# Root mean squares of a two-layer decoder step: column products and diagonals replaced by sums on all partitions

## The chip, the cores and the metric

The kernel runs on one core of one Trainium2 chip. The core has TensorE (PE, matrix products, results in PSUM), VectorE (DVE), ScalarE (ACT), GpSimd (POOL) and SyncE (SP, here only a queue that issues transfers). The metric is the device time of one execution in microseconds (us); lower is better.

## The reference, cut to what matters

Two layers are applied to a prompt of 1024 tokens and a sample group of 8 times 4 tokens, with a width of 1024. Each layer normalizes its input, computes one input projection, four branches (pooling, short convolution, Conformer convolution with a LayerNorm, differential attention with a norm per head), merges them, and ends in an output projection and a second norm. All norms need the same scalar for each token, one over the root of a mean square:

```python
def _rms(x, g):
    y = xf * lax.rsqrt(jnp.mean(xf * xf, axis=-1, keepdims=True) + EPS)
...
h = _rms(x, g_pre) * (1.0 + scale[:, None]) + shift[:, None]
y_c = jax.nn.silu(_layernorm(conv_c + b_cconv, g_cnorm, b_cnorm))
o = _rms(attend(q, k, v, lam), g_subln) * (1.0 - lam_init)
out = _rms(merged @ w_o, g_post)
```

## The kernel before, in words

Channels lie on the 128 partitions and tokens along the free axis, so a sum over channels runs over partitions. The 1056 tokens (1024 of the prompt, 32 of the samples) form three blocks of 352 (`TB`). A large product is 24 TensorE instructions of 128x128 by 128x352: each float32 operand is split into a high and a low part in the type float32r, and three of the four part products are summed over 8 slices of the depth (`gemm`, line 238). Results land in PSUM banks, two of them (`mm`) in the attention stages and five later, and an engine other than TensorE has to empty a bank before it is used again.

The function `drive` walks through the large products, weight unit by weight unit, three blocks each. Between them it steps generators that hold the rest: `attn` (one head of prompt attention), `decode` (two heads of sample attention), `pool`, `layernorm`. A scheduler then orders the instructions of each engine by its own estimate of durations; SP alone keeps the order of the program. Every engine works through its own row strictly in order.

`rstd_of(x, n, scale, dg, pb)` brings 1/sqrt(scale * sum + eps) of every token to all partitions. `x` holds, on each partition, partial sums of squares for `n` tokens. It is called in 38 places: 16 times at the end of the heads' attention (512 tokens each, two halves per head, line 646; I call the stretch from the last product with V to the end of these two roots an attention tail), 4 times in `decode` (64 tokens), 6 times in `layernorm` (352), 6 times behind the output projection (352, into the bank `ada`, line 1216), 3 times for the next layer's norm (352, line 1224) and 3 times at the start (`rstd_x`). It works in four steps:

- Line 349: products with the tokens as the stationary operand and one column of ones as the moving one, 4 for each call (1 in `decode`) in float32. The sums of up to 128 tokens lie on as many partitions, in a PSUM buffer `ms`, of which there are two. The trace shows each float32 product as two records.
- Lines 351 and 352: square root on ScalarE and reciprocal on VectorE, of at most 128x4 values. Lines 355 and 356 split the result into two float32r parts.
- Line 360: a diagonal matrix for each part, the identity times that column, on VectorE.
- Line 364: products of ones with the diagonals, two float32r products of the full number of columns (one float32 product in `decode` and at the start), which spread the values over all partitions, into a second `ms` buffer or into `ada`.

The caller then multiplies with the result in PSUM (lines 647, 792, 1098, 1219, and `norm_apply`). ScalarE also splits the weights (line 210) and empties banks (line 497 copies a key or query block in four pieces). It has to load another function table (`ACT_TABLE_LOAD`) when it changes between the square root and functions such as the exponential or the hyperbolic tangent. Line 1211 adds the squares behind the output projection on POOL, for the last slice on VectorE.

Of the kernel before, what the change touches and what calls it, by code (L numbers as in the profile page):

```python
# [13 lines left out]
AF = mybir.ActivationFunctionType  # L14
# [84 lines left out]
def step_kernel(ctx, tc, xT, wst, wada, kc, vc, ptab, stp, sts, stc, cT, vecs, wpool, lamqk, cst, rope,  # L99
# [58 lines left out]
    def ms(n=512):  # L158
        return psA("ms", 512)[:, 0:n]
# [161 lines left out]
    def make_A(l, k=0, n=KC):  # L321
        g = cv("g_pre", l, k, n).unsqueeze(2).to_broadcast([P, n, 9])
        ve.scalar_tensor_tensor(out=Am[:, k:k + n], in0=modT[l][:, 8 + k:8 + k + n], scalar=1.0, in1=g, op0=ALU.add, op1=ALU.mult)
# [18 lines left out]
    def rstd_of(x, n, scale, dg, pb=None):  # L342


        w = max(w_ for w_ in (P, TB // 4, 64) if n % w_ == 0)
        m = n // w
        pc = ms(m)[:w]
        for j in range(m):
            te.matmul(out=pc[:, j:j + 1], lhsT=x[:, j * w:(j + 1) * w], rhs=ones[:, 0:1], start=True, stop=True)  # L349
        r = const("rsm", 8, bufs=2)[:w, 0:m]  # L350
        sc.activation(out=r, in_=pc, func=AF.Sqrt, bias=epsc[:w], scale=scale)
        ve.reciprocal(out=r, in_=r)
        rs = [r] if len(dg) == 1 else [const(f"rsm{i}", 8)[:w, 0:m] for i in range(2)]
        if len(dg) == 2:
            ve.tensor_copy(out=R(rs[0]), in_=r)
            ve.tensor_tensor(out=R(rs[1]), in0=r, in1=rs[0], op=ALU.subtract)
        cast = R if len(dg) == 2 else lambda ap: ap
# [65 lines left out]
    def setup_lambda(l, lq):  # L423
# [9 lines left out]
        for o, name, f, w in ((0, "pool_scale", 0.5, 4), (4, "g_cnorm", 0.5, 4), (8, "b_cnorm", 0.5, 4),  # L433
                              (12, "g_subln", 0.5 * (1.0 - lam_init), 1)):
# [4 lines left out]
    def layer(l, pos, hh, hl, begun, psB):  # L439
# [120 lines left out]
        def attn(h):  # L560
# [91 lines left out]
        def decode(p):  # L652
# [137 lines left out]
            sqd, rsd = wn[:, 0:64], wn[:, 64:128]  # L790
# [650 lines left out]
```

## Time and profile before

| what | value |
|---|---|
| median of 3 runs | 3004.43 us (3002.55 to 3007.85) |
| the profiled execution's own time | 3002.23 us |
| its span, first to last instruction | 3000.4 us |
| TensorE busy | 2913.8 us, 97% of the span |
| weight loads of TensorE busy | 2781.6 us, 93% |
| VectorE, ScalarE, POOL busy | 1634.2, 970.6 and 495.1 us |
| granted TensorE clock, mean | 0.989 |

TensorE's row is nearly full, and each large product's instruction starts about 0.16 us after the one before it. A time saved on another engine counts only where TensorE waits for it. A TensorE instruction taken out of a full stretch moves everything behind it forward, unless the work behind it then has to wait for something else.

### The profile page before, as it was taken

How to read it: one execution, taken by the hardware profiler on the slowest of the kernel's cores; microseconds unless marked ns; L12 is line 12 of the kernel's file. 1: busy time of each engine (PE TensorE's matmuls, PEld its weight loads, DVE VectorE, ACT ScalarE, POOL GpSimd, SP SyncE). 2: the span in 40 equal slices, each digit the busy share in tenths (PEclk: the TensorE clock that was granted, in tenths of full speed). 3: DMA queues.
4: the chain of work that ended last, by engine and by line, in shares of the span. 5: the costliest groups of instructions: out<-in, count | busy, mean ns of one | idle time of the engine just before them, and what ended most of it. 6: DMA issues, size and time to landing. Idle time of an engine off the chain costs nothing.

```text
span 3000.4 us, 46185 instructions
## 1 busy us (share of the span) xinstructions
PE 2913.8 (97%) x18436; PEld 2781.6 (93%) x18436; DVE 1634.2 (54%) x2540; ACT 970.6 (32%) x1904; POOL 495.1 (17%) x642
## 2 busy tenths in 40 slices
PE   6999999999999999999989999999999999999998
PEld 4899889989999999999989998998899999999998
DVE  7756356577972145323487663664889522543233
ACT  4544245313112123212454551542221121322132
POOL 3221011012200111011230120101140001110123
PEclk8999999999999999999999999999999999999999
DMA  6122621362233223222321236115511221221122
GB/s 230 48 65 85 203 78 53 116 196 64 67 109 105 80 86 96 97 75 71 108 98 48 67 118 205 49 45 153 179 38 59 84 76 43 80 90 57 50 69 97
DMA packets 135961, 280.08 MB, mean 93 GB/s; under 512 B 18338, under 2 KB 88994, under 8 KB 134210
## 3 DMA queue, kind: packets, MB, share of 16 engines
q10 hardware_dynamic: 45072, 145.74, 15.9%
q1 hardware_dynamic: 79778, 90.73, 9.7%
q0 software_dynamic: 10896, 40.67, 3.6%
q8 instruction: 145, 2.38, 0.3%
q14 instruction: 70, 0.57, 0.1%
HBM read 240.73 MB, written 36.34 MB: 92 GB/s over the span
## 4 chain that ended last, share of the span: by engine, by line
PE 84%; DVE 7%; DMA 2%; issue 2%; SPq 2%; ACT 2%; POOL 0%; DVEq 0%; ACTq 0%; POOLq 0%
PE mm_t L238 45%; PE m_t L238 28%; PE s_t L238 3%; PE ms_t L238 2%; DVE acc_t L954 2%; SPq L671 1%; PE ms_t L611 1%; PE s_t L776 1%; DVE wlo_t L211 1%; PE s_t L702 1%; DVE acc_t L373 1%; DMA e_t<-in_kc_dram 1%; PE ms_t L349 1%; PE b_t L238 1%; ACT rop_t L497 1%
## 5 line engine op out<-in xcount | busy, mean ns | idle before, releaser
L238 PE MATMUL mm_t<-hh_t,whi_t 128*128 128x352 f32 x2792 | 533.3, 329 | 5.8 <-ACT hh_t L385 2.1
L238 PE MATMUL mm_t<-hh_t,wlo_t 128*128 128x352 f32 x2792 | 528.6, 327 | 0.0
L238 PE MATMUL mm_t<-hl_t,whi_t 128*128 128x352 f32 x2792 | 524.0, 325 | 0.0
L211 DVE TENSOR_TENSOR wlo_t<-wst_t,whi_t 128x1024 fp32r<-128x1024 f32 x203 | 268.5, 1329 | 455.6 <-ACT whi_t L210 455.4
L238 PEld LDWEIGHTS mm_t<-hh_t,whi_t 128*128 128x128 f32 x2792 | 458.7, 190 | 27.6 <-issue 14.6
L238 PEld LDWEIGHTS mm_t<-hh_t,wlo_t 128*128 128x128 f32 x2792 | 460.5, 189 | 9.7 <-issue 8.2
L238 PEld LDWEIGHTS mm_t<-hl_t,whi_t 128*128 128x128 f32 x2792 | 458.7, 189 | 6.7 <-issue 5.6
L954 DVE SCALAR_TENSOR_TENSOR acc_t<-uc_t,vec_t,acc_t 128x1024 f32<-128x1024 f32 x240 | 320.4, 1360 | 1.6
L1164 POOL TENSOR_TENSOR mg_t<-mg_t,th_t 128x352 f32<-128x352 f32 x144 | 144.7, 1008 | 925.8 <-DVE th_t L1163 925.7
L210 ACT ACTIVATE whi_t<-wst_t 128x1024 fp32r<-128x1024 f32 x203 | 213.3, 1056 | 246.7 <-PE mm_t L238 163.6
L238 PE MATMUL m_t<-hh_t,wlo_t 128*128 128x352 f32 x1352 | 249.7, 325 | 0.0
L238 PE MATMUL m_t<-hl_t,whi_t 128*128 128x352 f32 x1352 | 247.6, 324 | 0.0
L238 PE MATMUL m_t<-hh_t,whi_t 128*128 128x352 f32 x1352 | 246.4, 323 | 0.0
L238 PEld LDWEIGHTS m_t<-hh_t,wlo_t 128*128 128x128 f32 x1352 | 223.6, 190 | 0.9
L238 PEld LDWEIGHTS m_t<-hl_t,whi_t 128*128 128x128 f32 x1352 | 222.7, 189 | 0.0
L238 PEld LDWEIGHTS m_t<-hh_t,whi_t 128*128 128x128 f32 x1352 | 222.0, 189 | 0.1
L1072 ACT ACTIVATE th_t<-m_t 128x352 f32<-128x352 f32 x114 | 52.6, 463 | 373.4 <-PE m_t L238 362.5
L1072 ACT ACTIVATE th_t<-mm_t 128x352 f32<-128x352 f32 x78 | 35.9, 463 | 272.0 <-PE mm_t L238 240.9
L590 DVE TENSOR_REDUCE sml_t<-s_t 128x1 f32<-128x256 f32 (+7 forms) x128 | 92.4, 752 | 53.1 <-PE s_t L238 52.7
L593 ACT ACTIVATE e_t<-s_t,sml_t 128x256 f32<-128x256 f32 (+7 forms) x128 | 94.3, 744 | 69.7 <-DVE sml_t L591 39.9
L238 PE MATMUL m_t<-yh_t,whi_t 128*128 128x352 f32 x460 | 94.5, 326 | 0.0
L238 PE MATMUL m_t<-yh_t,wlo_t 128*128 128x352 f32 x460 | 93.1, 324 | 0.0
(349 smaller groups left out, 3854.0 us busy)
## 6 DMA issues: line engine op xcount, KB each, us to landing
wst_t<-in_wst_dram ACTq DMA_DIRECT2D x209, 512.0 KB, 3.6
e_t<-in_kc_dram SPq DMA_DIRECT2D x224, 128.0 KB, 3.0
e_t<-in_vc_dram SPq DMA_DIRECT2D x216, 128.0 KB, 2.6
rld_t<-ysp_t ACTq DMA_DIRECT2D x16, 528.0 KB, 4.5
wa_t<-in_wada_dram SPq DMA_DIRECT2D x16, 512.0 KB, 10.4
wlo_t<-in_wada_dram ACTq DMA_DIRECT2D x16, 512.0 KB, 3.7
whi_t<-in_wada_dram ACTq DMA_DIRECT2D x16, 512.0 KB, 4.3
x_t<-in_xT_dram SPq DMA_DIRECT2D x3, 1408.0 KB, 6.0
```

The source lines that it names most:

```text
L210: sc.activation(out=R(hi), in_=st, func=AF.Copy)
L211: (eng or ve).tensor_tensor(out=R(lo), in0=st, in1=hi, op=ALU.subtract)
L238: last_mm[0] = m = te.matmul(out=out, lhsT=R(lh), rhs=R(rh), start=first and i == 0, stop=last and i == n - 1)
L349: te.matmul(out=pc[:, j:j + 1], lhsT=x[:, j * w:(j + 1) * w], rhs=ones[:, 0:1], start=True, stop=True)
L373: ve.tensor_reduce(out=acc[:, i], in_=o.rearrange("p k n -> p n k"), axis=AX.X, op=ALU.add)
L497: sc.activation(out=sw[32 * (g ^ 1):32 * (g ^ 1) + 32], in_=pb[32 * g:32 * g + 32], func=AF.Copy)
L590: ve.tensor_reduce(out=s[:, j:j + 1], in_=S[j][:, :n], axis=AX.X, op=ALU.max)
L593: sc.activation(out=E[qb % 2][j][:, :n], in_=S[j][:, :n], func=AF.Exp, bias=s[:, 2 + j:3 + j], scale=0.125, accum_out=s[:, 4 + j:5 + j])
L611: te.transpose(out=pb[:, k], in_=e0[:, (k0 + k) * P:(k0 + k + 1) * P], identity=ident)
L954: pace(ve.scalar_tensor_tensor(out=a, in0=v, scalar=w(k), in1=a, op0=ALU.mult, op1=ALU.add))
L1072: sc.activation(out=th[:, b * TB:(b + 1) * TB], in_=pb, func=AF.Tanh, scale=0.5)
L1164: gp.tensor_tensor(out=mg[:, d, cl], in0=mg[:, d, cl], in1=th, op=ALU.add)
```

## The change

`rstd_of` no longer makes columns or diagonals. It scales the partial sums and splits them into a high part (ScalarE, line 353) and a low part (VectorE, line 354), and multiplies ones with both (two float32r products, line 356). That gives the mean square of each token on all partitions at once, in one PSUM buffer. In `decode` and at the start it is one float32 product with ones (line 358) and a scaling on VectorE (line 359). From there it works on the full 128 partitions: an estimate of one over the root on ScalarE (line 361, `Abs_reciprocal_sqrt`), its square on ScalarE (line 362), and a Newton step in two VectorE instructions in the PSUM buffer (lines 363 and 364). The step leaves -2 times the root; the factor -0.5 is folded into constants (`hv`, `Am`) or into the caller's multiplication, which becomes a `scalar_tensor_tensor` with the same operands. The two parts, the estimate and its square take tiles of their own; in attention they are the tiles e0 to e3 of the exponentials.

```diff
     def make_A(l, k=0, n=KC):
...
+        ve.scalar_tensor_tensor(out=a, in0=modT[l][:, 8 + k:8 + k + n], scalar=1.0, in1=g, op0=ALU.add, op1=ALU.mult)
+        ve.tensor_scalar(out=a, in0=a, scalar1=-0.5, scalar2=None, op0=ALU.mult)
...
-    def rstd_of(x, n, scale, dg, pb=None):
-        w = max(w_ for w_ in (P, TB // 4, 64) if n % w_ == 0)
-        m = n // w
-        pc = ms(m)[:w]
-        for j in range(m):
-            te.matmul(out=pc[:, j:j + 1], lhsT=x[:, j * w:(j + 1) * w], rhs=ones[:, 0:1], start=True, stop=True)
-        r = const("rsm", 8, bufs=2)[:w, 0:m]
-        sc.activation(out=r, in_=pc, func=AF.Sqrt, bias=epsc[:w], scale=scale)
-        ve.reciprocal(out=r, in_=r)
...
-        for r, d in zip(rs, dg):
-            d = d[:w].rearrange("p (j t) -> p j t", t=w)
-            ve.tensor_tensor(out=cast(d), in0=ident[:w, :w].unsqueeze(1).to_broadcast([w, m, w]),
-                             in1=r.unsqueeze(2).to_broadcast([w, m, w]), op=ALU.mult)
-        pb = ms(n) if pb is None else pb
-        for i, d in enumerate(dg):
-            te.matmul(out=pb, lhsT=cast(ones[:w]), rhs=cast(d[:w]), start=i == 0, stop=i == len(dg) - 1)
+    def rstd_of(x, scale, parts, yt, pb=None):
+        n = x.shape[-1]
+        y, t = yt
+        pb = ms(n) if pb is None else pb
+        if parts:
+            hi, lo = parts
+            sc.activation(out=R(hi), in_=x, func=AF.Copy, scale=scale)
+            ve.scalar_tensor_tensor(out=R(lo), in0=x, scalar=scale, in1=hi, op0=ALU.mult, op1=ALU.subtract)
+            for i in range(2):
+                te.matmul(out=pb, lhsT=R(ones), rhs=R(parts[i]), start=i == 0, stop=i == 1)
+        else:
+            te.matmul(out=pb, lhsT=ones, rhs=x, start=True, stop=True)
+            ve.tensor_scalar(out=pb, in0=pb, scalar1=scale, scalar2=None, op0=ALU.mult)
+        sc.activation(out=y, in_=pb, func=AF.Abs_reciprocal_sqrt, bias=epsc)
+        sc.activation(out=t, in_=y, func=AF.Square)
+        ve.scalar_tensor_tensor(out=pb, in0=pb, scalar=EPS, in1=t, op0=ALU.add, op1=ALU.mult)
+        ve.scalar_tensor_tensor(out=pb, in0=pb, scalar=-3.0, in1=y, op0=ALU.add, op1=ALU.mult)
         return pb
...
-                dg = ep(f"e{i}", 1024)
-                rs = rstd_of(msq[:, c], 512, 1.0 / P, two(dg.rearrange("p (i n) -> p i n", i=2)))
+                dg, yt = [ep(f"e{i + x}", 1024).rearrange("p (i n) -> p i n", i=2) for x in (0, 2)]
+                rs = rstd_of(msq[:, c], 1.0 / P, two(dg), two(yt))
...
-            rs = rstd_of(ssq, TB, 1.0 / D, two(op("acc", 2, TB)), psM("ada", 512)[:, 0:TB])
+            rs = rstd_of(ssq, 1.0 / D, two(op("parts", 2, TB)), two(op("yt", 2, TB)), psM("ada", 512)[:, 0:TB])
...
-                ve.tensor_tensor(out=o_, in0=o_, in1=rs.unsqueeze(1).to_broadcast([P, 2, TB]), op=ALU.mult)
+                ve.scalar_tensor_tensor(out=o_, in0=rs.unsqueeze(1).to_broadcast([P, 2, TB]), scalar=-0.5, in1=o_,
+                                        op0=ALU.mult, op1=ALU.mult)
```

The scheduler orders the new program anew. On TensorE in the attention tail of layer 0's first head, before the change (`ms_t` with `e_t` and `vl_t` is the last product with V; `mm_t` are large products; a row joins equal instructions):

```order
L238 MATMUL ms_t<-e_t,vl_t 128x256
L349 MATMUL ms_t<-ones_t,ms_t 128x1 x4
L238 MATMUL mm_t<-hh_t,whi_t 128x352 x6
L238 MATMUL mm_t<-hh_t,wlo_t 128x352 x8
L238 MATMUL mm_t<-hl_t,whi_t 128x352 x8
L238 MATMUL mm_t<-hh_t,whi_t 128x352 x8
L364 MATMUL ms_t<-e_t,ones_t 128x512
L349 MATMUL ms_t<-ones_t,ms_t 128x1 x2
L364 MATMUL ms_t<-e_t,ones_t 128x512
L349 MATMUL ms_t<-ones_t,ms_t 128x1 x2
L238 MATMUL mm_t<-hh_t,wlo_t 128x352 x8
L238 MATMUL mm_t<-hl_t,whi_t 128x352 x8
L238 MATMUL mm_t<-hh_t,whi_t 128x352 x8
```

and after it:

```order
L238 MATMUL ms_t<-e_t,vl_t 128x256
L356 MATMUL ms_t<-e_t,ones_t 128x512 x2
L238 MATMUL mm_t<-hh_t,whi_t 128x352 x3
L238 MATMUL mm_t<-hh_t,wlo_t 128x352 x8
L238 MATMUL mm_t<-hl_t,whi_t 128x352 x8
L238 MATMUL mm_t<-hh_t,whi_t 128x352 x8
L238 MATMUL mm_t<-hh_t,wlo_t 128x352 x2
L356 MATMUL ms_t<-e_t,ones_t 128x512
L238 MATMUL mm_t<-hh_t,wlo_t 128x352 x4
L356 MATMUL ms_t<-e_t,ones_t 128x512
L238 MATMUL mm_t<-hh_t,wlo_t 128x352 x2
L238 MATMUL mm_t<-hl_t,whi_t 128x352 x8
```

The column products are gone, the first half's two products stand right behind the product with V, and the second half's stand 29 and 33 instructions later.

On ScalarE in the same tail, before (`rsm_t` is the small root, `rop_t` the copy that empties a key block's bank):

```order
L623 ACTIVATE ms_t<-ms_t 128x256
L351 ACT_TABLE_LOAD
L351 ACTIVATE rsm_t<-ms_t,epsc_t 128x4
L497 ACTIVATE rop_t<-mm_t 32x352 x4
L351 ACTIVATE rsm_t<-ms_t,epsc_t 128x4
L506 ACTIVATE k_t<-rop_t 64x352 x2
L497 ACTIVATE rop_t<-mm_t 32x352 x4
```

and after:

```order
L623 ACTIVATE ms_t<-ms_t 128x256
L361 ACT_TABLE_LOAD
L361 ACTIVATE e_t<-ms_t,epsc_t 128x512
L353 ACTIVATE e_t<-ms_t 128x512
L362 ACTIVATE e_t<-e_t 128x512
L210 ACTIVATE whi_t<-wst_t 128x1024
L361 ACTIVATE e_t<-ms_t,epsc_t 128x512
L185 DMA wst_t<-in_wst_dram 128x1024
L362 ACTIVATE e_t<-e_t 128x512
L497 ACTIVATE rop_t<-mm_t 32x352 x8
```

The key block's four copies stood between the two small roots; now they stand behind both halves' estimates and squares and behind a weight split (line 210).

On TensorE where layer 1 begins, at the root for the last block of its input, before (`s_t` is a score, `acc_t` holds the sums of squares, then the diagonals):

```order
L238 MATMUL s_t<-maskr_t,identr_t 128x128
L238 MATMUL s_t<-kl_t,q_t 128x256 x2
L349 MATMUL ms_t<-ones_t,acc_t 88x1 x4
L364 MATMUL ms_t<-acc_t,ones_t 128x352
L526 MATMUL ms_t<-cs_t,vcm_t 128x128 x2
L364 MATMUL ms_t<-acc_t,ones_t 128x352
L526 MATMUL ms_t<-cs_t,vcm_t 128x128 x3
L238 MATMUL mm_t<-hh_t,whi_t 128x352 x15
```

and after:

```order
L238 MATMUL s_t<-maskr_t,identr_t 128x128
L238 MATMUL s_t<-kl_t,q_t 128x256 x2
L356 MATMUL ms_t<-parts_t,ones_t 128x352
L526 MATMUL ms_t<-cs_t,vcm_t 128x128 x2
L356 MATMUL ms_t<-parts_t,ones_t 128x352
L526 MATMUL ms_t<-cs_t,vcm_t 128x128 x3
L238 MATMUL mm_t<-hh_t,whi_t 128x352 x15
```

The column products are gone; the transposes of V (line 526) stand between the two products with ones as before, and the large products behind them wait for the normalized block in both.

## Rows read from the trace of the kernel before

**Rows 1.** The page: span, TensorE's busy time, the chain that ended last by line.
```profile
span 3000.4 us, 46185 instructions
PE 2913.8 (97%) x18436; PEld 2781.6 (93%) x18436; DVE 1634.2 (54%) x2540; ACT 970.6 (32%) x1904; POOL 495.1 (17%) x642
PE mm_t L238 45%; PE m_t L238 28%; PE s_t L238 3%; PE ms_t L238 2%; DVE acc_t L954 2%; SPq L671 1%; PE ms_t L611 1%; PE s_t L776 1%; DVE wlo_t L211 1%; PE s_t L702 1%; DVE acc_t L373 1%; DMA e_t<-in_kc_dram 1%; PE ms_t L349 1%; PE b_t L238 1%; ACT rop_t L497 1%
```

**Rows 2.** Waits of TensorE: who for whom, us in total, times, longest.
```profile
PE mm_t L300 <- DMA wa_t<-in_wada_dram: 12.4, 1, 12.4
PE s_t L702 <- DMA e_t<-in_kc_dram: 8.5, 6, 2.8
PE ms_t L349 <- DVE acc_t L374: 6.4, 2, 5.7
PE ms_t L526 <- ACT vcm_t L541: 6.1, 1, 6.1
```

**Rows 3.** Line 349: its weight loads, ns min/median/max, first and last start, form.
```profile
L349 PEld LDWEIGHTS ms_t<-ones_t,ms_t x128: 187/192/193, 162.6 to 2053.1; 128*128 128x128 f32 x128
L349 PEld LDWEIGHTS ms_t<-ones_t,ssq_t x48: 153/158/158, 1463.6 to 2986.9; 128*88 128x88 f32 x48
```

**Rows 4.** Timeline of TensorE, an attention tail: start us, us, engine, line.
```profile
162.70 0.95 PE L349 MATMUL ms_t<-ones_t,ms_t 128*128 128x1 f32 x8
163.51 1.22 PE L238 MATMUL mm_t<-hh_t,whi_t 128*128 128x352 f32 x6
164.56 1.46 PE L238 MATMUL mm_t<-hh_t,wlo_t 128*128 128x352 f32 x8
165.86 1.46 PE L238 MATMUL mm_t<-hl_t,whi_t 128*128 128x352 f32 x8
```

**Rows 5.** Timeline of TensorE, output projection of layer 0, block 0.
```profile
1463.80 0.71 PE L349 MATMUL ms_t<-ones_t,ssq_t 128*88 128x1 f32 x8
1464.38 0.57 PE L238 MATMUL mm_t<-hh_t,whi_t 128*128 128x352 f32 x2
1464.78 1.46 PE L238 MATMUL mm_t<-hh_t,wlo_t 128*128 128x352 f32 x8
```

**Rows 6.** Timeline of ScalarE in the attention tail of rows 4.
```profile
163.18 0.38 ACT L623 ACTIVATE ms_t<-ms_t 128x256 f32<-128x256 f32 x1
163.58 1.28 ACT L351 ACT_TABLE_LOAD   x1
164.87 0.26 ACT L351 ACTIVATE rsm_t<-ms_t,epsc_t 128x4 f32<-128x4 f32 x1
167.40 1.88 ACT L497 ACTIVATE rop_t<-mm_t 32x352 f32<-32x352 f32 x4 [2.26 <-issue]
```

**Rows 7.** Groups by line: busy us, mean ns, idle before them and its releaser.
```profile
L397 ACT ACTIVATE hh_t<-x_t,modT_t 128x352 fp32r<-128x352 f32 (+1 forms) x18 | 9.7, 569 | 8.5 <-DVE x_t L396 8.5
L1209 ACT ACTIVATE sq_t<-m_t 128x352 f32<-128x352 f32 x25 | 11.5, 459 | 0.0
L1092 DVE SCALAR_TENSOR_TENSOR lx_t<-ms_t,lx_t 128x1408 f32<-128x1408 f32 x6 | 9.7, 1620 | 0.0
L1098 DVE TENSOR_TENSOR lx_t<-lx_t,ms_t 128x1408 f32<-128x1408 f32 x6 | 9.7, 1617 | 0.4
L648 DVE SCALAR_TENSOR_TENSOR od_t<-od_t,hv_t,gd_t 128x512 f32<-128x512 f32 x16 | 12.7, 794 | 0.2
L360 DVE TENSOR_TENSOR e_t<-cs_t,rsm_t 128x512 fp32r<-128x512 f32 x32 | 22.2, 730 | 0.0
```

**Rows 8.** Timeline of TensorE where layer 1 begins.
```profile
1557.93 1.33 PE L349 MATMUL ms_t<-ones_t,acc_t 128*88 128x1 f32 x8 [5.72 <-DVE acc_t L374]
```

**Rows 9.** Timeline of the last root at the kernel's end.
```profile
2986.32 0.79 PE L349 MATMUL ms_t<-ones_t,ssq_t 128*88 128x1 f32 x8 [1.69 <-DVE ssq_t L1211]
2989.62 3.28 DVE L1219 TENSOR_TENSOR ob_t<-ob_t,ada_t 128x704 f32<-128x704 f32 x4 [0.75 <-PE ada_t L364]
```

**Rows 10.** Timeline of TensorE at the start, where the first large products begin.
```profile
36.46 1.25 PE L238 MATMUL b_t<-hh_t,whi_t 128*128 128x352 f32 x3 [4.26 <-ACT hh_t L397]
```

More of the change, by code (lines that the diff above doesn't have):

```diff
@@ L322, in make_A @@
         g = cv("g_pre", l, k, n).unsqueeze(2).to_broadcast([P, n, 9])
-        ve.scalar_tensor_tensor(out=Am[:, k:k + n], in0=modT[l][:, 8 + k:8 + k + n], scalar=1.0, in1=g, op0=ALU.add, op1=ALU.mult)
+        a = Am[:, k:k + n]
+        ve.scalar_tensor_tensor(out=a, in0=modT[l][:, 8 + k:8 + k + n], scalar=1.0, in1=g, op0=ALU.add, op1=ALU.mult)
+        ve.tensor_scalar(out=a, in0=a, scalar1=-0.5, scalar2=None, op0=ALU.mult)
     def make_G(l):
@@ L340, in two @@
         return [t[:, 0], t[:, 1]]
-    def rstd_of(x, n, scale, dg, pb=None):
-        w = max(w_ for w_ in (P, TB // 4, 64) if n % w_ == 0)
-        m = n // w
-        pc = ms(m)[:w]
-        for j in range(m):
-            te.matmul(out=pc[:, j:j + 1], lhsT=x[:, j * w:(j + 1) * w], rhs=ones[:, 0:1], start=True, stop=True)
-        r = const("rsm", 8, bufs=2)[:w, 0:m]
-        sc.activation(out=r, in_=pc, func=AF.Sqrt, bias=epsc[:w], scale=scale)
-        ve.reciprocal(out=r, in_=r)
[L353 to L357, printed above, removed]
-        for r, d in zip(rs, dg):
-            d = d[:w].rearrange("p (j t) -> p j t", t=w)
-            ve.tensor_tensor(out=cast(d), in0=ident[:w, :w].unsqueeze(1).to_broadcast([w, m, w]),
-                             in1=r.unsqueeze(2).to_broadcast([w, m, w]), op=ALU.mult)
-        pb = ms(n) if pb is None else pb
-        for i, d in enumerate(dg):
-            te.matmul(out=pb, lhsT=cast(ones[:w]), rhs=cast(d[:w]), start=i == 0, stop=i == len(dg) - 1)
+    def rstd_of(x, scale, parts, yt, pb=None):
+        n = x.shape[-1]
+        y, t = yt
+        pb = ms(n) if pb is None else pb
+        if parts:
[11 more added lines that the diff above has]
+        ve.scalar_tensor_tensor(out=pb, in0=pb, scalar=-3.0, in1=y, op0=ALU.add, op1=ALU.mult)
         return pb
@@ L789, in decode @@
             sc.activation(out=fin, in_=pb, func=AF.Copy)
-            sqd, rsd = wn[:, 0:64], wn[:, 64:128]
+            sqd, yd = wn[:, 0:64], wn[:, 64:128]
             sc.activation(out=sqd, in_=pb, func=AF.Square)
             yield
-            ve.tensor_tensor(out=fin, in0=fin, in1=rstd_of(sqd, 64, 1.0 / P, [rsd]), op=ALU.mult)
+            ve.tensor_tensor(out=fin, in0=fin, in1=rstd_of(sqd, 1.0 / P, None, (yd, qf)), op=ALU.mult)
             ve.scalar_tensor_tensor(out=fin, in0=fin, scalar=hv[:, l, 12:13],
@@ L1096, in layernorm @@
                 yield from skip(6)
-                rs = rstd_of(s2, TB, 1.0 / 512, [lnp("ls1", TB), lnp("ls3", TB)])
-                ve.tensor_tensor(out=x, in0=x, in1=rs.unsqueeze(1).to_broadcast([P, 4, TB]), op=ALU.mult)
+                rs = rstd_of(s2, 1.0 / 512, [lnp(f"lr{i}", TB) for i in range(2)], [t[:, i] for i in range(2)])
+                ve.scalar_tensor_tensor(out=x, in0=rs.unsqueeze(1).to_broadcast([P, 4, TB]), scalar=-0.5, in1=x,
+                                        op0=ALU.mult, op1=ALU.mult)
                 for c in range(4):
@@ L1222, in layer @@
                 gp.dma_start(out=xmid[b], in_=xb)
-                rs = rstd_of(sumsq(xb, ob, op("acc", 2, TB)), TB, 1.0 / D, two(op("acc", 2, TB)))
+                rs = rstd_of(sumsq(xb, ob, op("acc", 2, TB)), 1.0 / D, two(op("parts", 2, TB)), two(op("yt", 2, TB)))
                 for t, x in zip(nh, "hl"):
@@ L1259, in rstd_x @@
             a = accs[b]
-            pb = rstd_of(a[:, 0], TB, 1.0 / D, [a[:, 1]])
+            pb = rstd_of(a[:, 0], 1.0 / D, None, (a[:, 1], tx[:, 0]))
             sc.activation(out=a[:, 0], in_=pb, func=AF.Copy)
```

3 lines of the change are left out of this document (2 added, 1 removed).

## The prediction

> **What bounds the kernel now.** Read the page first [rows 1]: TensorE is busy for 2913.8 of 3000.4 us, so all its idle time is 87 us, and the chain that ended last runs over it almost everywhere. The narrow column products of line 349 alone hold 1% of that chain, some 30 us. Then read the waits of TensorE [rows 2]: the longest are a transfer at the start (12.4 us), page loads of the decode stage (8.5 us in six waits), the sums of squares where layer 1 begins (5.7 us), and one block of V at the start (6.1 us). So there are two kinds of places. In a full stretch the price of a step is the time that TensorE gives it; at the start, at the layer boundary and at the end the chain of steps counts. Of the 38 roots, 33 stand in full stretches, 3 at the start, one at the boundary, one at the end.
>
> **What goes, in full stretches.** One half of an attention tail has eight records of line 349. They start at 162.70, the next large product at 163.51: 0.81 us [rows 4]. The six instructions behind them take 1.05 us (163.51 to 164.56), where an undisturbed eight take 1.30 (164.56 to 165.86, so 0.1625 each, 0.975 for six): another 0.08. One half costs 0.89 us, and there are 16: 14.2 us. With 352 tokens the stationary operand has 88 columns instead of 128: 0.58 us from 1463.80 to 1464.38, and the next two take 0.40 instead of 0.325: 0.66 us [rows 5]. There are 13 of these in full stretches (6 of the LayerNorm, 5 of 6 behind the output projection, 2 of 3 for the next layer's norm): 8.5 us. The 8 records of the decode stage, at the 0.11 us of an attention record, give 0.9. The sum is **23.6 us**. The two products with ones stay as they are in number and columns, so nothing comes back on TensorE. Without the slower restart it would be 21.3; that is the lower bound. The upper one is the chain's 30 us, which holds the start and the end as well.
>
> Why are products with one moving column so dear? The rows show the weight loads at 192 ns for 128 columns and 158 ns for 88 [rows 3], overlapping at a pitch of 0.101 and 0.073 us (0.81 and 0.58 over eight), so the pitch follows the stationary columns. The Trainium skill ("TensorE: Matmul & The Clock Gate", section "Back-to-back issue gap") gives moving sizes of 1 to 64 columns an isolated floor of about 25 ns; by that the 240 records would be worth 6 us and the result would be near 3004. Its section "LDWEIGHTS" gives columns/1.2 ns, 107 and 73 ns, and the trace agrees with this one.
>
> **What comes, on ScalarE and VectorE.** No row shows the new root over 512 columns. ScalarE takes 380 ns for 256 columns [rows 6] and 459 for 352, and 569 for 352 with a bias tile [rows 7]; on that line a copy or square of 512 takes 0.59 us and the estimate with its bias 0.70. The lower bound is the 0.46 of 352 columns, the upper 0.9 (twice 459 ns). I take 0.59 and 0.70, since the line runs through measured sizes. Per half that is 0.59 + 0.70 + 0.59 less the small root of 0.26 [rows 6]: +1.6 us, +3.2 per tail. VectorE gets three instructions of 0.79 (line 648's price) for two diagonals of 0.73 and three small ones [rows 7]: at most +0.9 per half. A PSUM operand adds nothing: 1620 ns for a scalar_tensor_tensor and 1617 for a tensor_tensor, both with one [rows 7], which also prices the callers' exchange of the latter for the former at zero. All of this lies beside TensorE as long as banks are emptied in time. The number of table loads stays, 46 in either order.
>
> **Is the cover thick enough?** Take the tail of rows 4, with zero at the end of the last product with V. TensorE: two wide products to 0.5, 29 large ones to 5.2, the high part, four large, the low part to 6.3, then the rest of the first key block to 7.9 and the second to 11.8. There it needs the bank that the first one filled. ScalarE: two evictions to 0.9, table load of 1.28 [rows 6] to 2.2, first estimate 2.9, second high part 3.5, square 4.1, a weight split; the second estimate has to wait for the product at 6.3, and ends at 7.1, its square at 7.7. The first key block's four copies (1.88 us [rows 6]) follow from 8.1 to 10.0. VectorE finishes the second half's Newton step near 9.5, multiplies, and is done with the bank near 11.3. So the bank is free some 0.5 us early. The cover is thin, and queued behind the waiting estimate are a weight transfer, a square and eight key copies; whoever waits for those is TensorE. I charge 0.25 us per tail, **+2 us** for eight; the bounds are 0 and 1.1 us per tail (0 and 9), the latter if one estimate and one square come on top of the slack.
>
> **The three exposed places.** At the end, the last root runs from 2986.32 to 2989.62, 3.30 us [rows 9]. The new chain has 0.46 (high part), 0.55 (low part, 794 ns scaled to 352 columns), about 0.4 for the last product, 0.57, 0.46 and two times 0.55, with some 0.3 of hand-overs: 3.8. That is **+0.5** (bounds 0 and +1). At the boundary TensorE waits for the sums already [rows 8]. The same +0.5 applies, and by the new order key and query work stands between the estimate and its square on ScalarE and ahead of both Newton instructions on VectorE, about as much again; the projection's root ahead of it ends later by like amounts: **+1.8** in all (bounds 0 and +4). At the start three groups of column products go, 2.0 us at 0.66 each [rows 5], but the first large product waits for VectorE and ScalarE [rows 10], where three instructions per block replace two small ones and the weight splits now stand between the constant `Am` and its new scaling: **+1.5** (bounds -2, if the products bound it, and +4, if all of the new instructions do).
>
> **Sum.** -23.6 + 2 + 0.5 + 1.8 + 1.5 = -17.8 us. The profiled execution took 3002.23 us (span 3000.4 and 1.8 around it), so 2984.4 for its like. It lies 2.2 us below the median of the runs; on that footing the forecast is **2986.5 us**.
>
> **Rivals.** *The gain is waited away*: TensorE arrives earlier at page loads, weight loads and banks. For it: waits for pages exist [rows 2], and the thin cover above. Against it: all waits for transfers other than the first are below 15 us in 3000. If half of what full stretches gain is lost, 11.8 us, the time is 3004.4 - 17.8 + 11.8 = 2998. *Slower*: the bank of the first key block becomes the limit in every attention tail. Beyond 0.5 us of slack, each microsecond by which the copies of line 497 come late costs 8 us. Against the 19.8 us which all else gains, the point of no change is 0.5 + 19.8/8 = 3.0 us of lateness, and slower by 0.2% (6 us) starts at 3.7. If all that ScalarE gains (3.2), VectorE gains (1.8) and the table load (1.28) ended up ahead of the copies, it is 6.3 late: 5.8 x 8 = 46, and 3004.4 - 19.8 + 46 = 3031; half of that lateness, near the decision point, gives 3006. I put this case at 3012. The Trainium skill ("TensorE: Matmul & The Clock Gate", section "Architectural detail") calls ScalarE and VectorE strict FIFOs with TensorE alone pulling loads ahead; that is the mechanism of this case, and rows 6 agree in that the copies come after both the load and the small root. *More than forecast*: in attention, the tile e1 that the page loads wait for comes free right behind the low part at 6.3 us instead of after the diagonals, so the 8.5 us of page waits [rows 2] shrink, and the exposed chains cost nothing: 3004.4 - 23.6 - 5 = 2976. *It does not do what it says*: excluded as to TensorE, since the new order has no column product left.
>
> **Chances and range.** Forecast 0.66, waited away 0.17, more 0.10, slower 0.07. The forecast's own range, from its bounds, is 2979 to 2996. The range that should hold 8 in 10 takes in the larger gain in part and most of the waiting case: 2975 to 2999. About 0.2% is what a measurement of this kernel can tell from no change, that is below 2998.4 for faster and above 3010.4 for slower. Faster: 0.66 + 0.10 + 0.07 of the waiting case = 0.83. Same: the other 0.10. Slower: 0.07.
>
> **What would show it.** Right: TensorE's instructions fall by 280 records and its busy time by some 25 us; its share of the span stays at 97%; line 349 has left the chain; in attention tails the large products follow the products with ones without idle time. Wrong: new waits of TensorE for line 497, 498 or 842 in attention tails of over 1 us each (the slower case), waits for page or weight transfers that grow by ten microseconds in all (waited away), or a first large product later than 39 us at the start. The forecast fails if the new order leaves TensorE idle in places that the roots don't touch, which the order alone cannot tell.

## The result and the profile after

The changed kernel takes 2977.93 us (median, 2976.93 to 2983.99) against 3003.49 us for the kernel before on the same chip: a ratio of 0.9917, 95% interval 0.9900 to 0.9934, that is 20 to 30 us less. A second measurement on another occasion gave 2981.06 us, ratio 0.9927 (0.9911 to 0.9942). The forecast was 2986.5 us, 18 us less; the first measurement lies just below the forecast's own range of 2979 to 2996, the second inside it. The profiled execution has a span of 2975.2 us, 25.2 less than that of [rows 1].

The page of the changed kernel: span, busy time of each engine with its share and instructions, the last chain by line.

```profile
span 2975.2 us, 45643 instructions
...
PE 2883.2 (97%) x18156; PEld 2754.0 (93%) x18156; DVE 1640.4 (55%) x2488; ACT 1015.9 (34%) x1973; POOL 502.1 (17%) x642
...
PE mm_t L238 16%; PE m_t L238 14%; SPq L671 1%; DVE acc_t L954 1%; PE s_t L238 1%; PE ms_t L238 1%; DVE wlo_t L211 0%; SPq L409 0%; PE s_t L776 0%; DMA lx_t<-csp_t 0%; DMA e_t<-in_kc_dram 0%; DMA csp_t<-lx_t 0%; PE ms_t L611 0%; PE s_t L702 0%; ACT L361 0%
```

TensorE has 280 records less, as forecast, and is busy 30.6 us less; its idle time (span less busy) rises from 86.6 to 92.0 us. Line 349 is gone from the chain, but the chain of this page covers only some 40% of the span (that of [rows 1] nearly all), so its other shares cannot be compared. ScalarE is busy 45 us more; what that costs is in the waits for banks below.

TensorE's waits, to be held against [rows 2] (us in total, times, longest):

```profile
PE b_t L238 <- ACT hh_t L397: 8.3, 1, 8.3
PE ms_t L356 <- ACT parts_t L353: 8.0, 2, 7.8
PE ms_t L238 <- ACT dh_t L1021: 6.7, 3, 3.1
...
PE mm_t L238 <- DVE rop_t L498: 4.3, 5, 1.2
PE ms_t L238 <- DVE wpl_t L977: 3.8, 2, 2.1
PE s_t L702 <- DMA e_t<-in_kc_dram: 3.6, 5, 1.0
PE ms_t L1091 <- DVE ls_t L1088: 2.2, 2, 1.5
...
PE mm_t L238 <- DVE bth_t L850: 1.5, 2, 0.7
...
PE s_t L702 <- DMA od_t<-in_kc_dram: 1.2, 2, 0.7
```

The kernel before has three lines that [rows 2] leave out, the first of them its second longest wait in total:

```profile
PE ms_t L238 <- ACT dh_t L1021: 11.3, 3, 5.3
...
PE ms_t L1091 <- DVE ls_t L1088: 3.1, 3, 1.7
...
PE mm_t L238 <- DVE rop_t L498: 1.1, 1, 1.1
```

The waits for the tiles `e_t` of key pages fell from 8.5 to 3.6 us. The waits for banks that lines 498 and 850 empty are new in the attention stages: the 1.1 us of before stood at 1547 us, at the layer boundary. The 7.8 us at the layer boundary stand where 5.7 and 1.4 us stood. The waits for `dh_t` belong to the pooling branch. They fell from 11.3 to 6.7 us, but those for `wpl_t` (3.8 us) came in their place.

Where the difference arises is seen by counting the large products (128x352 into the banks `mm` and `m`; each kernel has 15,456 records of them) and setting the start of the same one in both traces side by side (the number is that of the records ahead of it):

| record | place | before, us | after less before, us |
|---|---|---|---|
| 72 | start over | 86.3 | +0.4 |
| 144 | first heads | 99.1 | +5.9 |
| 3672 | attention of layer 0 over | 843.2 | -6.6 |
| 5184 | before the LayerNorm | 1098.1 | -6.8 |
| 5760 | behind it | 1203.1 | -9.8 |
| 7200 | before the output projection | 1443.4 | -9.9 |
| 7776 | boundary | 1542.2 | -12.9 |
| 7920 | layer 1 begun | 1586.8 | -11.6 |
| 11232 | attention of layer 1 over | 2294.8 | -24.9 |
| 14976 | before the last projection | 2904.7 | -23.9 |
| 15408 | its last block | 2976.7 | -25.9 |

So the two LayerNorms and output projections gave 3.0, 0.0, 3.0 and 2.0 us, and the attention stages of the two layers (86 to 843 and 1587 to 2295 us) 7.0 and 13.2, where the forecast had 14.2 + 0.9 - 2 = 13.1 for both together. The 3.0 us of layer 0's LayerNorm and the 0.0 of layer 1's are the work of a wait, that for the LayerNorm's own sums (line 1088): in layer 0 it was 2.8 us and is gone, in layer 1 it rose from 0.4 to 2.2 us and took the gain of the column products back.

### The profile page after: what moved, and what is told of

Read it like the earlier page. It is cut to its first block, busy times and chain, and to the rows that moved or that the text cites. A ratio compares the mean times of both kernels' runs of the same rounds, so it can differ in the third digit from the quotient of the medians.

```text
span 2975.2 us, 45643 instructions
## 1 busy us (share of the span) xinstructions
PE 2883.2 (97%) x18156; PEld 2754.0 (93%) x18156; DVE 1640.4 (55%) x2488; ACT 1015.9 (34%) x1973; POOL 502.1 (17%) x642
## 3 DMA queue, kind: packets, MB, share of 16 engines
q10 hardware_dynamic: 45072, 145.74, 15.7%
## 5 line engine op out<-in xcount | busy, mean ns | idle before, releaser
L238 PE MATMUL m_t<-yl_t,whi_t 128*128 128x352 f32 x460 | 93.3, 324 | 0.0
```

Of the source, the lines that this page charges most:

```text
L238: last_mm[0] = m = te.matmul(out=out, lhsT=R(lh), rhs=R(rh), start=first and i == 0, stop=last and i == n - 1)
```

## Is it TensorE's own time? Column products put back

In the changed kernel, dead column products ahead of the products with ones:

```diff
+        w = max(w_ for w_ in (P, TB // 4, 64) if n % w_ == 0)
+        for j in range(n // w):
+            te.matmul(out=pb[:w, j:j + 1], lhsT=x[:, j * w:(j + 1) * w], rhs=ones[:, 0:1], start=True, stop=True)
         if parts:
```

> The changed kernel with the column products put back as dead work: ahead of the two products with ones, the same 280 records in float32 write into columns that the first product with ones then overwrites. Nothing waits for them, the other engines do what they do in the changed kernel. Theory (the gain is TensorE's own time of these records, 0.81 us for eight with 128 columns, 0.58 with 88, and the slower restart behind them): 26 us of records, 2 of restarts, so 24 to 28 us more than the changed kernel's 2977.9, about 3003. Rival (the gain came from earlier page loads and another order, and the records mostly lay beside other work): at most 12 us more, below 2990. At 25 ns a record it would be 6 us more, 2984.

Measured: 3008.13 us, ratio to before 1.0012 (1.0002 to 1.0023). From 0.9917 or 0.9927 this is 25 to 29 us more. Nothing waits for these products, no other engine has an instruction more, and the whole gain is gone. The weight loads of the put-back records, by line (ns min/median/max):

```profile
L353 PEld LDWEIGHTS ms_t<-ones_t,ms_t x128: 187/192/192, 161.7 to 2054.1; 128*128 128x128 f32 x128
...
L353 PEld LDWEIGHTS ms_t<-ones_t,acc_t x48: 152/158/272, 22.0 to 1556.3; 128*88 128x88 f32 x48
```

Their medians are those of [rows 3], and a record costs about 0.1 us (25 to 29 over 280). The Trainium skill ("TensorE: Matmul & The Clock Gate", section "Back-to-back issue gap") gives 25 ns as the floor between isolated products of up to 64 moving columns, and adds that the isolated gap leaves out the weight loads. Taken as the price of each record, that floor is an estimate of 7 us in all; the measurement excludes it.

## The parts: attention tails alone, norms alone

The new root in the 16 attention halves of the kernel before (`rstd_new` is the function of the changed kernel):

```diff
-                dg = ep(f"e{i}", 1024)
-                rs = rstd_of(msq[:, c], 512, 1.0 / P, two(dg.rearrange("p (i n) -> p i n", i=2)))
+                dg, yt = [ep(f"e{i + x}", 1024).rearrange("p (i n) -> p i n", i=2) for x in (0, 2)]
+                rs = rstd_new(msq[:, c], 1.0 / P, two(dg), two(yt))
```

> The kernel before with the new root in the 16 halves of the attention tails alone (same tiles as in the changed kernel); the other 22 roots and the constants are those of before. Theory: the forecast's terms for the tails are 14.2 us of TensorE time less 2 us of waits for banks, and 6 to 7 us more come from the decode stages, whose page loads start 6 us earlier behind the product with V: 18 to 20 us below before, 2984 to 2986. Rival (the page waits have nothing to do with the tails): 12 us below before, 2992. Second rival (nearly all of the change's gain sits here, and the LayerNorm and the output projection give nothing): 24 to 26 us below, 2978 to 2980.

Measured: 2986.15 us, ratio 0.9947 (0.9933 to 0.9962), 17 us below before: nearest to the theory's time, but not by its cause, as TensorE's waits show:

```profile
PE s_t L725 <- DMA e_t<-in_kc_dram: 6.9, 3, 2.4
...
PE mm_t L238 <- DVE rop_t L521: 4.1, 5, 1.1
...
PE s_t L725 <- DMA od_t<-in_kc_dram: 2.0, 2, 1.2
PE s_t L799 <- DMA e_t<-in_vc_dram: 2.0, 3, 1.4
```

With 10.9 us in these lines the waits for pages are hardly shorter than the 12.3 of before, though the loads start earlier (lines 725, 799 and 521 are 702, 776 and 498 here). The account below finds 17.4 us in TensorE's own work instead, where the forecast had 14.2 for these tails.

The complement without the decode stages and the start:

```diff
-                rs = rstd_of(msq[:, c], 1.0 / P, two(dg), two(yt))
+                rs = rstd_old(msq[:, c], 512, 1.0 / P, two(dg.rearrange("p (i n) -> p i n", i=2)))
...
-            ve.tensor_tensor(out=fin, in0=fin, in1=rstd_of(sqd, 1.0 / P, None, (yd, qf)), op=ALU.mult)
+            ve.tensor_tensor(out=fin, in0=fin, in1=rstd_old(sqd, 64, 1.0 / P, [rsd]), op=ALU.mult)
```

> The kernel before with the new root in the LayerNorm, behind the output projection and for the next layer's norm alone, 15 of the 38 places; attention tails, decode stages and the start are those of before. Theory: 13 places in full stretches at 0.66 are 8.6 us, the boundary costs 1.2 and the end 0.5, as the trace of the changed kernel shows them: 6 to 8 us below before, 2996 to 2998, and together with the 17 us of the attention tails alone that is the whole change. Rival (where the trace shows no gain, as in the LayerNorm of layer 1, the products' time has turned into a wait for the LayerNorm's own sums): 4 to 5 us below, 2999.

Measured: 2996.54 us against 3004.06, ratio 0.9969 (0.9957 to 0.9981): 7.5 us less by the medians, 9 by the ratio, where the theory said 6 to 8. The two parts sum to 0.84%, the whole change measured 0.83 and 0.73%. So the parts add up, and the sum of the norms' terms was right. The rival's mechanism is there too, in layer 1, where this run waits 2.6 us for line 1088's counterpart; the wait that is gone in layer 0 makes up for it, which nobody had forecast.

## Do earlier page loads explain the rest?

The trace of the changed kernel suggested it: in the second head's tail the page loads start 0.9 us behind the start of the last product with V (278.74 and 277.86 us) where they started 7.1 us behind it (282.75 and 275.68), and TensorE's waits for pages (lines 702 and 776) fall from 12.3 to 5.1 us. In the profile of the second measurement, of the same program, they are 7.5 us, so 2.4 us of such a difference can be chance. Four edits, in five runs, ask it in different ways.

The tiles exchanged in the changed kernel:

```diff
-                dg, yt = [ep(f"e{i + x}", 1024).rearrange("p (i n) -> p i n", i=2) for x in (0, 2)]
+                dg, yt = [ep(f"e{i + x}", 1024).rearrange("p (i n) -> p i n", i=2) for x in (2, 0)]
```

> The changed kernel with the tiles of the attention halves exchanged: estimate and square in e0 and e1, the two parts in e2 and e3. The cache pages that the decode stage needs are loaded into e0 first and e1 second, in the order of the program, so the first page load has to wait for the first half's Newton step, and the second for the second half's, as in the kernel before it waited for the diagonals' products. Theory (page waits fell by 7.3 us, from 13.0 to 5.7, because e0 and e1 come free behind the products with ones): page waits of 10 to 14 us again, the time 5 to 8 us above the changed kernel, 2983 to 2986. Rival (the waits fell by chance of the new order): within 2 us of 2977.9.

Measured: 2980.99 us, ratio 0.9926 (0.9913 to 0.9940), no different from the changed kernel. The loads did start some 7 us behind the product with V again, but the waits did not come back:

```profile
PE ms_t L722 <- DVE qf_t L720: 4.9, 2, 2.5
...
PE s_t L702 <- DMA e_t<-in_kc_dram: 2.1, 3, 1.3
```

In the new order the first decode products stand 26 to 28 us behind the product with V instead of 20 to 23, and TensorE waits at line 722 instead. The theory fell here. That distance does not explain the waits either: in the kernel before it was 23 to 26 us, with 12.3 us of waits.

In the kernel before, the diagonals moved to other tiles:

```diff
-                dg = ep(f"e{i}", 1024)
+                dg = ep(f"e{i + 2}", 1024)
```

> The kernel before with one edit: the diagonals of the attention halves in e2 and e3 instead of e0 and e1. No work is added or taken away. The first two page loads can then start at the end of the heads, some 6 us earlier, and two more wait for the diagonals. Theory (page loads behind the tiles of the roots cost TensorE waits): page waits of 13.0 us fall to 6 to 9, the time 4 to 7 us below before, 2996.5 to 2999.5. Rival (e3 and e2 are the tiles that the first decode products read, so the waits stay or grow): 3003 to 3007.

Measured: 2994.49 us, ratio 0.9969 (0.9957 to 0.9982): 9 us less with no work removed, more than the theory's 4 to 7. The waits for pages fell from 12.3 to 7.4 us, as the theory said:

```profile
PE s_t L702 <- DMA e_t<-in_kc_dram: 4.9, 4, 1.4
...
PE s_t L776 <- DMA e_t<-in_vc_dram: 2.0, 2, 1.2
```

So in this kernel the pages are about half of the gain. And the analogous step in the changed kernel:

```diff
-                dg, yt = [ep(f"e{i + x}", 1024).rearrange("p (i n) -> p i n", i=2) for x in (0, 2)]
+                dg, yt = [ep(f"e{x}", 1024).rearrange("p (i n) -> p i n", i=2) for x in ((3, 2), (5, 7))[i]]
```

> The changed kernel with other tiles for the attention halves: e3 and e2 in the first half, e5 and e7 in the second, so that e0 and e1, which the page loads take first, come free before the product with V and the roots hold only tiles that are loaded later. Theory (early page loads are what moves the decode stage; the same step in the kernel before gave 9.6 us): page loads start some 20 us earlier, TensorE's waits for pages of 5.7 us go to 2 or 3, and the time is 3 to 6 us below the changed kernel, 2972 to 2975. Rival (the changed kernel has taken this gain already): within 2 us of 2977.9.

Measured: 2994.39 us, ratio 0.9977 (0.9964 to 0.9991): 13 us more than the changed kernel beside it, the opposite sign. Key page loads started 14 to 17 us earlier, counted from the last product with V, and TensorE's waits for key pages were 2.1 us, so the loads themselves did what was meant. The loss is elsewhere, first in waits that the changed kernel does not have:

```profile
PE mm_t L238 <- ACT sg_t L909: 7.7, 2, 4.4
PE ms_t L722 <- DVE qf_t L720: 4.8, 2, 2.4
```

The windows show the rest. Columns: stretch, its length, busy us (instructions) of PE, PEld, DVE, ACT and POOL, TensorE's granted clock, DMA. The kernel before, in the attention stages:

```profile
105.00:770.00 665.00, 655.61 (x4297) 610.92 (x4295) 420.32 (x739) 251.28 (x544) 106.40 (x166) 1.00 0.33 100
770.00:790.00 20.00, 14.72 (x83) 14.43 (x82) 20.00 (x21) 3.19 (x6) 2.22 (x2) 0.91 0.18 53
...
2060.00:2080.00 20.00, 17.17 (x102) 14.86 (x101) 2.69 (x4) 1.41 (x2) 2.04 (x5) 0.91 0.76 228
...
2255.00:2275.00 20.00, 14.69 (x77) 14.40 (x78) 20.00 (x22) 3.73 (x7) 4.80 (x4) 0.83 0.17 51
```

The changed kernel:

```profile
690.00:705.00 15.00, 12.95 (x70) 12.65 (x70) 12.81 (x15) 4.38 (x7) 5.88 (x7) 0.89 0.13 45
...
2235.00:2250.00 15.00, 12.20 (x66) 11.91 (x65) 15.00 (x17) 3.73 (x7) 3.33 (x3) 0.89 0.29 97
```

And the one with the late tiles:

```profile
290.00:300.00 10.00, 7.91 (x43) 5.22 (x42) 5.64 (x9) 4.51 (x9) 3.76 (x6) 0.83 0.87 265
...
570.00:590.00 20.00, 14.24 (x83) 12.11 (x83) 6.75 (x12) 5.71 (x8) 3.02 (x10) 0.83 0.78 246
...
775.00:790.00 15.00, 9.69 (x52) 9.40 (x51) 14.96 (x17) 3.93 (x7) 4.06 (x3) 0.89 0.34 105
...
2050.00:2070.00 20.00, 13.21 (x71) 10.97 (x70) 4.68 (x9) 3.89 (x6) 2.28 (x7) 0.74 0.72 235
...
2250.00:2270.00 20.00, 15.65 (x86) 15.12 (x86) 19.93 (x24) 4.38 (x8) 4.26 (x4) 0.91 0.26 80
```

In every one of these stretches TensorE had idle time, and in a part of each the granted clock was at the lower of its two levels. Length times the missing share of the clock is 7.0 us before (20 x 0.09 twice and 20 x 0.17), 3.3 after, and 13.8 with the late tiles. Part of that falls into idle time. Counted only while TensorE was busy, and over the attention stages as a whole, the clock cost 11.4 us with the late tiles and 4.9 in the changed kernel beside it; idle time was 36.9 and 29.3 us. So the loss is about half clock and half waits.

A cheaper page load in both kernels:

```diff
-                    for j, (b, pg) in enumerate(pages_):
+                    for j, (b, pg) in enumerate(pages_[:1]):
                         r = page(b * NPG + pg)
-                        sp.dma_start(out=buf[:, j * 256:(j + 1) * 256],
-                                     in_=cache[l][bass.ds(r, 1), p].rearrange("a p n -> p (a n)"))
+                        sp.dma_start(out=buf.rearrange("p (j n) -> p j n", j=4),
+                                     in_=cache[l][bass.ds(r, 1), p].rearrange("a p n -> p a n").to_broadcast([P, 4, 256]))
```

> The kernel before with a quarter of the page loads: each tile of the decode stage takes one page four times in one transfer instead of four pages in four transfers, so three quarters of the cache are left out of the result. The bytes that land are the same, the time that the queue spends on issuing falls to a quarter. Theory (13.0 us of TensorE's waits are for pages, and they follow from the late start of these loads): the waits fall below 3 us, the time is 8 to 12 us below before, 2991 to 2996. Rival (the place of the decode products in the order decides, the pages are in time anyway): within 3 us of 3003.5.

> The changed kernel with the same edit (three quarters of the cache left out of the result). Theory: 5.7 us of waits for pages were left, so 3 to 6 us below the changed kernel, 2972 to 2976; against the run beside it without page waits the change is then worth 17 to 20 us, what the forecast's own terms give. Rival (the gain beyond the forecast has nothing to do with pages): 22 to 25 us stay between these two.

Measured: before with it 2997.92 us (ratio 0.9981, 0.9972 to 0.9990), after with it 2986.50 (0.9941, 0.9927 to 0.9954). The waits for pages did not vanish in either:

```profile
PE s_t L702 <- DMA gd_t<-in_kc_dram: 4.6, 2, 2.6
...
PE s_t L702 <- DMA e_t<-in_kc_dram: 4.1, 4, 1.5
```

These are the waits of the changed kernel with cheap loads. In the kernel before, the cheap loads left 9.6 us where 12.3 were. The changed kernel became slower, and the pair differs by 11 us, less than either expectation. Three quarters fewer issues do not buy off the waits. So the pages are not the cause in the sense I gave: neither an earlier start of the loads nor fewer of them brings the waits down reliably. That the new order, which places the decode products anew after each edit, decides it is an argument that no run here isolates.

## The cover and the start

The square of line 362 made twice in the attention halves:

```diff
-        sc.activation(out=t, in_=y, func=AF.Square)
+        for _ in range(squares):
+            sc.activation(out=t, in_=y, func=AF.Square)
```

> The changed kernel with the square of line 362 made twice in every attention half, dead work of 0.62 us on ScalarE, 1.24 us per tail. In the tail at 163 us the first key block's bank comes free some 0.5 us before TensorE needs it, and in four other tails TensorE already waits for the copies of line 498 (3.5 us in all). Theory (the cover is that thin): the tails that wait already get the full 1.2 us, the others what is over 0.5 us, together 5 to 8 us: 2983 to 2986. Rival (the copies can be late without harm, since the order is made anew and the scheduler puts them ahead of the squares): below 2 us, 2976 to 2980.

Measured: 2983.04 us, ratio 0.9936 (0.9921 to 0.9950), 2 us above the changed kernel beside it (2981.06), within the uncertainty of both. The time lies in the theory's band, the difference at the rival's bound, so the run does not decide between them. Of 9.9 us more on ScalarE the waits for the banks got 1.1:

```profile
PE mm_t L238 <- DVE rop_t L499: 5.4, 6, 1.4
```

The opposite edit takes the squares off ScalarE, with the start of before:

```diff
-        sc.activation(out=t, in_=y, func=AF.Square)
+            gp.tensor_tensor(out=t, in0=y, in1=y, op=ALU.mult)
```

> The changed kernel with the start of before (as in the run with that start) and, in the attention halves, the square on GpSimd, which is busy for 17% of the span. ScalarE has 1.24 us less in each tail. Theory (TensorE's 4 us of waits for the banks that line 498 empties follow from ScalarE's extra work): they fall below 2 us, the time is 2 to 4 us below the run with the start of before (2977.2), 2973 to 2975. Rival (the second square on ScalarE cost 2 us in 9.9, so the order absorbs such work either way): 2976 to 2979.

Measured: 2989.73 us, ratio 0.9953 (0.9939 to 0.9966), far from both expectations. The waits for the banks did fall to 0.5 us, and the time rose by some 12 us all the same: the mean granted clock fell from 0.989 to 0.987 and TensorE's idle time rose from 92.8 to 97.6 us, at other places (4.0 us of waits for `sg_t` are new). A wait that was taken away at its place did not shorten the program. The version with the start of before was:

```diff
-            pb = rstd_of(a[:, 0], 1.0 / D, None, (a[:, 1], tx[:, 0]))
+            r = const("rsm", 8, bufs=2)[:w, 0:4]
+            sc.activation(out=r, in_=pc, func=AF.Sqrt, bias=epsc[:w], scale=1.0 / D)
...
+            pb = ms(TB)
+            te.matmul(out=pb, lhsT=ones[:w], rhs=a[:w, 1], start=True, stop=True)
...
-        ve.tensor_scalar(out=a, in0=a, scalar1=-0.5, scalar2=None, op0=ALU.mult)
+        if l: ve.tensor_scalar(out=a, in0=a, scalar1=-0.5, scalar2=None, op0=ALU.mult)
```

> The changed kernel with the three roots at the start and the constant Am of layer 0 as in the kernel before; up to the first attention tail the order of the instructions on TensorE and ScalarE is then the one of before. In the changed kernel the 144th large product starts 5.9 us later than before (99.1 to 105.0 us), 0.8 of it from the roots themselves (the products at 79 us) and 5.1 from a new order of the first key block's copies and two stretches at half clock. Theory: it is not given back later, so 4 to 6 us below the changed kernel, 2972 to 2974. Rival (the lost time is made up at the page and weight transfers behind it): within 1.5 us of 2977.9.

Measured: 2977.20 us, ratio 0.9913 (0.9899 to 0.9927), the same as the changed kernel. The start itself was repaired (the 144th large product starts 0.1 us later than before instead of 5.9), but of the 4.8 us that it still led the changed kernel by at 139 us 3.2 were left at 580 us and none at 666: they went in the decode stage between the two. So what the start loses is given back later. The repeated measurement of the changed kernel stands beside these:

> The changed kernel itself, to stand beside the other three on the same chip. Every theory expects what was measured: 2977.9 us, ratio 0.9917 to before, within 2 us.

Measured: 2981.06 us, ratio 0.9927, 3 us above the first.

## One account for all of them

Each profile gives the span and TensorE's busy time; the difference is its idle time. The trace also records when the granted clock was at the lower of its two levels, half of the upper. The lost clock is half of the time in which TensorE was busy at the lower level, and TensorE's own work is its busy time less that. The sums over the low stretches, first of the kernel before (68.0 us low, 39.9 of them busy), then of the changed kernel:

```profile
sum 68.02, PE 39.87; mean PE 5.70
```

```profile
sum 61.41, PE 30.42; mean PE 3.80
```

| kernel | ratio | span | idle | lost clock | own work |
|---|---|---|---|---|---|
| before | 1 | 3000.4 | 86.6 | 19.9 | 2893.9 |
| before, diagonals in e2, e3 | 0.9969 | 2990.7 | 78.9 | 20.1 | 2891.7 |
| before, cheap pages | 0.9981 | 2994.6 | 81.2 | 19.3 | 2894.1 |
| before, new root in the tails | 0.9947 | 2980.9 | 87.9 | 16.5 | 2876.5 |
| before, new root in the norms | 0.9969 | 2994.9 | 89.2 | 19.6 | 2886.1 |
| after | 0.9917 | 2975.2 | 92.0 | 15.2 | 2868.0 |
| after, again | 0.9927 | 2978.9 | 95.0 | 15.7 | 2868.2 |
| after, tiles exchanged | 0.9926 | 2976.8 | 91.7 | 19.7 | 2865.4 |
| after, start of before | 0.9913 | 2975.2 | 92.8 | 16.0 | 2866.4 |
| after, two squares | 0.9936 | 2986.6 | 97.9 | 19.9 | 2868.8 |
| after, cheap pages | 0.9941 | 2981.0 | 89.9 | 22.0 | 2869.1 |
| after, squares on GpSimd | 0.9953 | 2988.0 | 97.6 | 23.1 | 2867.3 |
| after, late tiles | 0.9977 | 2992.5 | 101.4 | 22.9 | 2868.2 |
| after, columns put back | 1.0012 | 3002.7 | 85.0 | 19.7 | 2898.0 |

The own work is 2892 to 2894 us with the old root and 2865 to 2869 with the new one, whatever the edit: the change takes 26 us from it. The tails alone take 17.4, the norms alone 7.8, and the put-back columns bring 30, 4 more than the change took; those 4 I can't assign. All else, 107 to 124 us of idle time and lost clock in the changed kernels, moves with the order that each edit brings about.

## Why the prediction was right, point by point

**TensorE's own time: right.** The forecast's 23.6 us for the full stretches, with 0.66 each for the five exposed calls (the start's three, the boundary, the end), is 26.9 of own work; the account gives 25.9 and 25.7 in the two profiles of the changed kernel, and the columns put back cost 25 to 29 us. The parts are less exact than the sum: 17.4 for 14.2 in the tails, 7.8 for 9.9 in the 15 norms. Behind the product with V the large products follow at once, as it said they would (timeline of TensorE, the tail of rows 4):

```profile
163.46 0.62 PE L356 MATMUL ms_t<-e_t,ones_t 128*128 128x512 f32 x2
163.92 0.65 PE L238 MATMUL mm_t<-hh_t,whi_t 128*128 128x352 f32 x3
164.41 1.46 PE L238 MATMUL mm_t<-hh_t,wlo_t 128*128 128x352 f32 x8
```

**ScalarE's and VectorE's prices right, the cover's price too small.** ScalarE in that tail, then VectorE with the first key block's bank, then TensorE at its next use:

```profile
165.63 0.69 ACT L361 ACTIVATE e_t<-ms_t,epsc_t 128x512 f32<-128x512 f32 x1
166.22 0.62 ACT L353 ACTIVATE e_t<-ms_t 128x512 fp32r<-128x512 f32 x1
166.74 0.62 ACT L362 ACTIVATE e_t<-e_t 128x512 f32<-128x512 f32 x1
...
171.47 0.63 ACT L362 ACTIVATE e_t<-e_t 128x512 f32<-128x512 f32 x1 [0.86 <-DVE wlo_t L211]
172.13 1.89 ACT L497 ACTIVATE rop_t<-mm_t 32x352 f32<-32x352 f32 x4
```

```profile
174.21 0.52 DVE L498 TENSOR_TENSOR rop_t<-mm_t,cos_t 128x352 f32<-128x352 f32 x1
```

```profile
175.21 1.46 PE L238 MATMUL mm_t<-hh_t,whi_t 128*128 128x352 f32 x8
```

The estimate takes 0.69 and the square 0.62 us (taken: 0.70 and 0.59), VectorE's instructions 0.69 (taken: 0.79). The bank is free at 174.73 and needed at 175.21: 0.48 us early, where the walk through the tail had 0.5. In two of the eight tails, behind the second head of each layer, TensorE waits for line 498, 3.5 us in all, and in two more for line 850, 1.5: together 5.0 for the forecast's 2, within its bounds of 0 and 9. Two of these waits are 1.2 us long, over the 1 us that was named as a sign of the slower case; but that case needed 3.7 us of lateness in every tail, and was far.

**Start: its term right, what came after it not seen.** The first large product moved from 36.46 [rows 10] to 37.92 us, +1.46 for +1.5, within the 39 us that was named; at the 72nd record 0.4 of it is left. The lines of TensorE that then went wrong:

```profile
37.92 3.64 PE L238 MATMUL b_t<-hh_t,whi_t 128*128 128x352 f32 x10 [8.27 <-ACT hh_t L397]
...
93.92 2.40 PE L238 MATMUL mm_t<-hh_t,whi_t 128*128 128x352 f32 x8 [0.80 <-DVE rop_t L498]
96.11 2.20 PE L238 MATMUL mm_t<-hh_t,wlo_t 128*128 128x352 f32 x8
```

Eight products take 2.2 us instead of the 1.3 of an undisturbed stretch: behind the waits for a late key bank the granted clock was 0.79 and 0.78 from 92 to 96 and 96 to 100 us. The run with the old start shows no cost in the end (0.9913 against 0.9917 and 0.9927).

**Boundary and end: right.** 1.2 us between records 7776 and 7920, for 1.8. At the end the root runs from 2960.34 to 2964.35 us, 4.01 where [rows 9] had 3.30: +0.7 for +0.5.

```profile
2960.34 0.50 ACT L353 ACTIVATE parts_t<-ssq_t 128x352 fp32r<-128x352 f32 x1 [0.66 <-DVE ssq_t L1212]
...
2964.35 3.28 DVE L1220 SCALAR_TENSOR_TENSOR ob_t<-ada_t,ob_t 128x704 f32<-128x704 f32 x4
```

**What failed: the step that let all other waits, and the clock, stand.** The sum charged waits only where the roots themselves stand, 26.9 of own work less 17.8 of gain, about +9.1 us. The first profile of the changed kernel has +5.4 of idle time and -4.7 of lost clock, together +0.7; the second has +8.4 and -4.2, together +4.2. With 25.9 and 25.7 of own work that is 25.2 and 21.5 us of span for the forecast's 17.8. The clock was not in the sum at all, and gave more than 4 us in both; 3.2 of them lie ahead of the 72nd record, where TensorE is idle 4.9 us longer and less of its work falls into stretches at the lower level. The waits of the attention stages were in the sum with 2 us more. There the idle time fell by 3.0 and 0.3 us: pages gave 7.2 and 4.8, the banks took 5.8 and 5.7, the rest is small. Reading [rows 2], the prediction also passed over the 11.3 us for `dh_t`; that was harmless, since the pooling branch's waits stayed at 14 to 15 us in all.

The rival of a larger gain named the pages and put the time at 2976, but its cause, tiles that come free sooner, did not hold: tiles freed late left the waits low, tiles freed sooner helped one kernel and hurt the other. So the nearness of 2977.93 to that figure is luck. What remains shown is that orders of the same work differ by 13 us (late tiles and the changed kernel beside it, 2994.39 and 2981.06), and that the change drew one of the good ones. Which instruction of the order decides is open.

**The gain waited away: not here.** It is not in the changed kernel, but with the late tiles (0.9977) two thirds of it are gone. The rival exists, at a price of 13 us, and not by waits for pages but by idle time elsewhere and the lost clock behind it.

## To carry to other kernels

In a stretch that one engine fills, count that engine's instructions and take their price from the pitch between neighbours: here a product with a single moving column costs 0.1 us with 128 stationary columns and 0.07 with 88, so here the price followed the width of the stationary operand. Where a scheduler makes the order again after every edit, add to such a sum a term of either sign for the order, and get its size from edits that change no work (here 9 us less to 13 us more); a single wait in the trace is no proof of what the edit that removes it will bring. Compare edits by own work, idle time and lost clock apart, since the first stays within 4 us here where the whole time does not.

## What had not been expected of the hardware

TensorE's clock is a large part of what disturbs this kernel, 15 to 23 us of lost work beside 79 to 101 us of idle time. In the three kernels whose windows stand above, every stretch at the lower level in those windows begins during a wait of 2.1 to 5.3 us or less than 1 us behind it, so that the wait is paid once as idle time and again as slower products. This is one of them in the changed kernel, ahead of the low part of its window from 690 us:

```profile
694.48 0.60 PE L238 MATMUL ms_t<-dh_t,wpl_t 128*128 128x352 f32 x2 [2.06 <-DVE wpl_t L977]
```

Not every such wait is followed by one: the changed kernel's 3.1 us for `dh_t`, at 768 us, is not. And moving dead data to another tile, with no work changed, was worth 9 us (2994.49 against 3004.14).
